# The instruction scheduler's timing model, in a float32 encoder on one core

## The chip, the cores and the metric

The kernel runs on one core of one Trainium2 chip. The metric is the device time of one execution in microseconds; smaller is better. The core has five instruction streams that run side by side and wait for one another through semaphores: PE (TensorE, matmuls; its weight loads are shown apart as PEld), DVE (VectorE), ACT (ScalarE), POOL (GpSimd) and SP (SyncE, which here issues most DMA transfers). Each stream is carried out strictly in the order in which the compiled program has it: an instruction that waits holds up all behind it on its engine.

## The reference

Two pre-norm residual layers over 512 tokens with 1024 features in float32, on a grid of 8 by 64 tokens. Layer 0 has grouped-query attention and latent attention side by side, layer 1 a neighbourhood attention with a window of 8 by 16 tokens. Each layer ends with an MLP of 4096 hidden features:

```python
for layer in range(DEPTH):                       # DEPTH = 2
    hn = rmsnorm(h, norm_mix[layer])
    if layer % 2 == 0:
        h = h + hybrid_attention(hn, ...)        # 8 + 8 heads, full softmax over 512 keys
    else:
        h = h + neighbourhood_attention(hn, ...) # 16 heads, gathered keys, learned bias
    u = jax.nn.relu(rmsnorm(h, norm_ffn[layer]) @ w_up)
    h = h + (u * u) @ w_down
return rmsnorm(h, final_norm)
```

## The kernel before

The residual stream is kept transposed on the chip as `hT` (features on the partitions, 8 blocks of 128 by 512 tokens). Every float32 operand of a matmul is split in two: a high part in the matmul's own format (`fp32r`), made by ACT, and the rest, made by DVE (or POOL) as a difference. A product of two such operands is three matmuls: high by high, high by rest, rest by high (`mm3` at lines 501 to 503). Weights come through `chunk` (line 183 on): SP loads a `raw` tile, ACT writes `whi` (line 212), DVE writes `wlo` (line 202). `weights` keeps up to five loads and two splits ahead of the matmul that asks for them.

The stages in the order of time are these:

- The projection of layer 0's inputs (`use_w`), with the norms, statistics and rotations that lead to the first heads (`ev_ka`, `ev_va`, `ev_q`, lines 593 to 710).
- `attend` for 16 heads in four blocks of 128 queries each: scores into a bank (line 997), a reduction on DVE (1001), an exponential on ACT (1003), a reciprocal on DVE (1004), a scaling on POOL (1005), transposes on PE (972), their split by ACT and DVE (974, 975), the product with the values (985). Between the steps `fill.run` writes pieces of other projections into the program, so many microseconds' worth a step.
- The output projection, then `mlp(0)`. A part of the MLP is done by products with seven multiplications in place of eight (class `Seven`): POOL forms sums of weight blocks (302 to 304), ACT and DVE split them (308, 309), PE multiplies (388 to 390), DVE combines the banks (397 to 400). The converse sums and splits of the activations (336 to 340, 362, 363) are written between the matmuls of the neighbouring products.
- `valuesC`, `projC` and `attend_C`, layer 1's attention, with the same kind of fillers.
- The output projection, `mlp(1)` with the last norm (`last_mlp`), and the stores.

The Python code writes one long list of instructions. As the `TileContext` closes, the framework turns it into the order of each engine. Its scheduler replays the list on a timing model: each time an engine comes free in the replay, it takes the earliest written instruction of that engine whose inputs, buffers and semaphores are ready in the replay at that moment. The order so found is the order that the chip executes. The semaphores are put in afterwards, so a wrong order costs waiting time, not correctness.

Three things limit the scheduler. The large slots (`a0` to `a29`) are taken and given back in Python, so which tile follows which in a slot is fixed as written. `tc.keep_in_program_order` (lines 630, 1184 and 1244) puts an instruction behind everything written before it on its engine: the conversions of activations in the MLPs are held so. And `attend_C` is written within

```python
return tc.manual_schedule(engines={mybir.EngineType.PE, mybir.EngineType.Activation, mybir.EngineType.DVE,
                                   mybir.EngineType.Pool})
```

which keeps the written order on four engines; SP's DMA issues are free there too. The pools with several buffers (`raw`, `whi`, `wlo`, `sc`, `p`, `ti`, and the eight PSUM banks under `mm`, `s`, `t`, `o`) are handed out as the replay reaches their users.

## Time and profile before

| | us |
|---|---|
| three runs | 1182.31, 1183.46, 1184.22 (median 1183.46) |
| profiled execution, first to last instruction | 1184.0 |
| PE idle in it, by stretches of the trace: 0 to 50 | 1.38 |
| 50 to 160 (end of the projection, start of the first attention) | 9.71 |
| 160 to 260 | 0.45 |
| 260 to 660 (first MLP, start of layer 1) | 0.23 |
| 660 to 820 (second attention) | 0.64 |
| 820 to 1080 (output projection, most of the second MLP) | 0.00 |
| 1080 to 1110 | 2.23 |
| 1110 to 1184 | 8.91 |

The profile's span runs from the first to the last instruction of one execution. A busy time is the union of an engine's instructions; matmuls overlap in the pipeline, so PE's busy time also holds slower stretches, which show in the distance between the starts of matmuls. In a row of the timeline stand the start, the time taken, the engine, the source line, the operation, the tile written and the tiles read with their shapes, the count, and in brackets how long the engine was idle before and what ended that.

### The profile page before, as it was taken

The page shows a single profiled execution, that of the slowest core. Times are in us where ns is not written, and L with a number is a line of the kernel's source. Part 1 is how long each engine was busy: PE and PEld are TensorE (multiplying, and loading weights), DVE is VectorE, ACT ScalarE, POOL GpSimd, SP SyncE. Part 2 cuts the span into 40 slices and gives each one's busy share as a digit, 9 for nine tenths or more (in the row PEclk, how much of TensorE's full clock was granted, in tenths as well). Part 3 has the DMA queues.
Part 4 walks back from the last instruction along what each step waited for, and adds up shares of the span by engine and source line. Part 5 has one row for each costly group of instructions (what it writes and reads, how often), then busy time and mean ns, then how long its engine had stood idle before and what let it go on. Part 6 is the DMA issues. An engine that isn't in the chain of part 4 may idle for free.

```text
span 1184.0 us, 19784 instructions
## 1 busy us (share of the span) xinstructions
PE 1160.5 (98%) x7128; PEld 1021.2 (86%) x7128; DVE 883.2 (75%) x1514; ACT 640.3 (54%) x1081; POOL 526.1 (44%) x662
## 2 busy tenths in 40 slices
PE   9989999999999999999999999999999999999997
PEld 8667778888899899988998998988889989998895
DVE  5788998878967368786884676667996736778975
ACT  4468676664546247562553565555554624666344
POOL 3267343224562377819602232231376625774710
PEclk9999999999999999999999999999999999999998
DMA  7223225212524723225226464433352341322412
GB/s 244 71 54 92 68 78 134 62 56 77 167 86 134 263 70 90 72 90 165 67 72 178 131 184 126 116 112 109 107 165 76 115 134 55 98 64 89 143 36 71
DMA packets 110145, 128.01 MB, mean 108 GB/s; under 512 B 9075, under 2 KB 86816, under 8 KB 110048
## 3 DMA queue, kind: packets, MB, share of 16 engines
q1 hardware_dynamic: 106992, 119.30, 33.5%
q0 software_dynamic: 2304, 6.31, 2.2%
q8 instruction: 56, 0.92, 0.3%
q10 hardware_dynamic: 752, 1.15, 0.3%
q14 instruction: 41, 0.34, 0.1%
HBM read 104.32 MB, written 6.29 MB: 93 GB/s over the span
## 4 chain that ended last, share of the span: by engine, by line
PE 81%; DVE 4%; ACT 1%; issue 1%; POOL 0%; DVEq 0%; ACTq 0%
PE mm L503 8%; PE mm L501 8%; PE mm L502 8%; PE mm L390 4%; PE mm L389 4%; PE mm L388 4%; PE t L388 3%; PE t L389 3%; PE t L390 3%; PE s L502 2%; PE s L503 2%; PE s L501 2%; PE s L390 2%; PE s L388 2%; PE s L389 2%; PE s L997 2%
## 5 line engine op out<-in xcount | busy, mean ns | idle before, releaser
L309 DVE TENSOR_TENSOR wlo<-a,whi 128x896 fp32r<-128x896 f32 x132 | 161.8, 1230 | 83.7 <-ACT whi L308 82.9
L308 ACT ACTIVATE whi<-a 128x896 fp32r<-128x896 f32 x132 | 125.0, 950 | 155.0 <-PE o L502 45.8
L501 PE MATMUL mm<-a,whi 128*128 128x512 f32 x485 | 195.9, 406 | 0.9 <-DVE a L915 0.7
L503 PE MATMUL mm<-a,wlo 128*128 128x512 f32 x485 | 192.1, 397 | 2.5 <-DVE wlo L202 2.5
L502 PE MATMUL mm<-a,whi 128*128 128x512 f32 x485 | 192.5, 397 | 0.1
L202 DVE TENSOR_TENSOR wlo<-raw,whi 128x1024 fp32r<-128x1024 f32 (+4 forms) x117 | 139.3, 1193 | 66.4 <-ACT whi L212 63.9
L212 ACT ACTIVATE whi<-raw 128x1024 fp32r<-128x1024 f32 (+3 forms) x120 | 116.4, 971 | 92.2 <-PE s L502 39.8
L302 POOL TENSOR_TENSOR a<-a 128x128 f32<-128x128 f32 x132 | 85.1, 645 | 173.3 <-DMA a<-in_ffn_w_up_dram 103.9
L303 POOL TENSOR_TENSOR a<-a 128x256 f32<-128x256 f32 x132 | 120.2, 910 | 10.3
L304 POOL TENSOR_TENSOR a<-a 128x128 f32<-128x128 f32 x132 | 115.1, 872 | 10.3
L503 PEld LDWEIGHTS mm<-a,wlo 128*128 128x128 f32 x485 | 91.7, 189 | 23.7 <-DVE wlo L202 3.4
L501 PEld LDWEIGHTS mm<-a,whi 128*128 128x128 f32 x485 | 91.8, 189 | 20.4 <-PE t L972 0.9
L502 PEld LDWEIGHTS mm<-a,whi 128*128 128x128 f32 x485 | 91.9, 190 | 17.4 <-DVE a L545 0.4
L388 PE MATMUL mm<-a,whi 128*128 128x256 f32 x370 | 103.9, 281 | 0.0
L389 PE MATMUL mm<-a,whi 128*128 128x256 f32 x370 | 103.9, 281 | 0.0
L390 PE MATMUL mm<-a,wlo 128*128 128x256 f32 x370 | 103.7, 280 | 0.0
L1005 POOL TENSOR_SCALAR p<-p,ti 128x512 f32<-128x512 f32 x64 | 46.2, 724 | 92.3 <-DVE ti L1004 81.1
L1430 POOL TENSOR_SCALAR p<-p,ti 128x256 f32<-128x256 f32 x64 | 35.6, 567 | 104.8 <-DVE ti L1429 91.8
L388 PE MATMUL t<-a,whi 128*128 128x256 f32 x264 | 74.2, 281 | 0.0
L389 PE MATMUL t<-a,whi 128*128 128x256 f32 x264 | 74.1, 281 | 0.0
L390 PE MATMUL t<-a,wlo 128*128 128x256 f32 x264 | 73.9, 280 | 0.0
L390 PEld LDWEIGHTS mm<-a,wlo 128*128 128x128 f32 x370 | 69.6, 188 | 0.2 <-DVE wlo L309 0.2
(338 smaller groups left out, 3210.8 us busy)
## 6 DMA issues: line engine op xcount, KB each, us to landing
a<-in_ffn_w_up_dram SPq DMA_DIRECT2D x104, 256.0 KB
raw<-in_ffn_w_down_dram SPq DMA_DIRECT2D x46, 512.0 KB
raw<-in_od_w_qkv_dram SPq DMA_DIRECT2D x64, 128.0 KB
a<-in_ffn_w_down_dram SPq DMA_DIRECT2D x28, 256.0 KB
raw<-in_ffn_w_up_dram SPq DMA_DIRECT2D x12, 512.0 KB
raw<-in_ev_w_in_dram SPq DMA_DIRECT2D x12, 384.0 KB
a<-a SPq DMA_DIRECT2D x18, 256.0 KB
bias<-bx SPq DMA_DIRECT2D x16, 256.0 KB
```

Source lines behind the costliest of these rows:

```text
L202: z = lambda: (eng or DVE).tensor_tensor(to, src, f32(high), op=ALU.subtract)
L212: ACT.activation(hi[:, 0:m], raw[:, 0:m], AF.Copy)
L303: POOL.tensor_tensor(r[:, 4:6], r[:, 2:3].to_broadcast([P, 2, P]), r[:, 0:7:6], op=ALU.add)
L304: POOL.tensor_tensor(r[:, 7], r[:, 3], r[:, 5], op=ALU.subtract)
L308: ACT.activation(hi[:, 0:896], raw[:, 128:1024], AF.Copy)
L309: DVE.tensor_tensor(lo[:, 0:896], raw[:, 128:1024], f32(hi[:, 0:896]), op=ALU.subtract)
L388: PE.matmul(o, wh, x[:, 0], start=kp == 0 and n in (0, 1, 3, 5), stop=False, skip_group_check=True)
L389: PE.matmul(o, wh, x[:, 1], start=False, stop=False, skip_group_check=True)
L390: PE.matmul(o, wl, x[:, 0], start=False, stop=kp == self.np - 1, skip_group_check=True)
L501: PE.matmul(o, wh, xh, start=first, stop=False)
L502: PE.matmul(o, wh, xl, start=False, stop=False)
L503: PE.matmul(o, wl, xh, start=False, stop=last)
```

## The change

One argument of the `TileContext` is set:

```diff
-    with tile.TileContext(nc) as tc:
+    with tile.TileContext(nc, schedule_with_timeline_sim=True) as tc:
         encoder_kernel(tc, aps, out)
```

Without it the scheduler replays the program on the framework's plain simulator of a core; with it, on the framework's timeline simulator, the more detailed of its two timing models. The written list, the pins, the hand-ordered stretch, the tiles and the instructions stay the same; the order of the instructions on each engine may differ wherever it is not pinned, and with it the order in which buffers of a pool are handed out.

## The prediction

> **What bounds the kernel now.** I read the page first, then the busy time by stretches, then what TensorE (PE) waited for, then the timelines around the longest of those waits.
>
> ```profile
> span 1184.0 us, 19784 instructions
> ...
> PE 1160.5 (98%) x7128; PEld 1021.2 (86%) x7128; DVE 883.2 (75%) x1514; ACT 640.3 (54%) x1081; POOL 526.1 (44%) x662
> ...
> PE 81%; DVE 4%; ACT 1%; issue 1%; POOL 0%; DVEq 0%; ACTq 0%
> ```
>
> PE works nearly all the time and carries most of the chain that ended last. No instruction is added or removed, so its work stays; only its 23.5 us of idle time (1184.0 - 1160.5) and what follows from idling can change. The next view says where that idle time lies: span of the stretch, then busy us and instructions of each engine, then the granted clock.
>
> ```profile
> 0.00:50.00 50.00, 48.62 (x235) 40.15 (x236) 29.28 (x60) 23.69 (x36) 14.19 (x21) 1.00 0.50 166
> 50.00:160.00 110.00, 100.29 (x548) 77.09 (x547) 95.76 (x236) 79.43 (x168) 57.06 (x59) 0.98 0.31 78
> 160.00:260.00 100.00, 99.55 (x572) 83.73 (x571) 83.11 (x180) 67.22 (x139) 30.28 (x39) 1.00 0.27 77
> 260.00:660.00 400.00, 399.77 (x2564) 361.64 (x2563) 293.94 (x399) 197.39 (x275) 199.77 (x252) 1.00 0.39 119
> 660.00:820.00 160.00, 159.36 (x982) 140.59 (x981) 108.29 (x290) 89.84 (x214) 44.27 (x79) 1.00 0.47 133
> 820.00:1080.00 260.00, 260.00 (x1665) 235.45 (x1664) 192.90 (x235) 138.56 (x184) 146.49 (x174) 1.00 0.33 102
> 1080.00:1110.00 30.00, 27.77 (x116) 22.25 (x115) 28.54 (x39) 10.97 (x16) 19.16 (x22) 0.94 0.32 97
> 1110.00:1184.00 74.00, 65.09 (x460) 60.28 (x459) 51.36 (x80) 33.21 (x55) 14.94 (x19) 0.96 0.23 71
> ```
>
> Of the idle time 9.71 us lie between 50 and 160 us (end of the first projection, start of the first attention), 2.23 between 1080 and 1110 (second MLP), 8.91 behind 1110 (nearly all the last output chain) and 1.38 ahead of 50 (first loads). The two long stretches from 260 to 660 and from 820 to 1080, the MLPs, idle 0.23 us together. The reader is to see that the MLPs can lose much and gain nothing, while the first attention can do either.
>
> **The change, part by part.** The scheduler replays the written program on a timing model. Whenever an engine comes free in that replay, it gets the earliest written instruction whose inputs and buffers are ready there. The change replaces the model, so what moves is which instruction counts as ready, on PE, ACT, DVE, POOL and on SP's DMA issues. Nothing else moves: the slots a0 to a29 are dealt out in the written order, the calls at lines 630, 1184 and 1244 pin some instructions behind the ones written before them, and the second attention (660 to 820) holds the order of its four engines by hand.
>
> *What can be gained.* PE's own waits:
>
> ```profile
> PE s L997 <- DVE ti L1001: 2.9, 2, 2.4
> PE mm L503 <- DVE wlo L202: 2.5, 2, 2.2
> PE t L597 <- POOL sc L595: 1.4, 3, 0.8
> PE s L997 <- DVE a L624: 1.4, 1, 1.4
> ```
>
> These are places where the present order puts an instruction ahead of its inputs. A model nearer to the chip would put other matmuls there. A wait also costs clock behind it; the two longest ones show that:
>
> ```profile
> 74.61 0.76 PE L997 MATMUL s<-a,a 128*128 128x512 f32 x2 [2.39 <-DVE ti L1001]
> ...
> 76.45 0.63 PE L503 MATMUL mm<-a,wlo 128*128 128x512 f32 x1
> 76.87 0.63 PE L501 MATMUL mm<-a,whi 128*128 128x512 f32 x1
> 77.30 0.63 PE L502 MATMUL mm<-a,whi 128*128 128x512 f32 x1
> ```
>
> ```profile
> 1099.72 0.39 PE L501 MATMUL mm<-a,whi 128*128 128x512 f32 x1
> 1099.95 0.40 PE L502 MATMUL mm<-a,whi 128*128 128x512 f32 x1
> 1102.58 0.79 PE L503 MATMUL mm<-a,wlo 128*128 128x512 f32 x1 [2.23 <-DVE wlo L202]
> 1103.17 0.63 PE L501 MATMUL mm<-a,whi 128*128 128x512 f32 x1
> ...
> 1105.73 0.52 PE L501 MATMUL mm<-a,whi 128*128 128x512 f32 x1
> ```
>
> Matmuls of 512 columns start 0.23 us apart before the wait and 0.43 after it. At 1102.58 the wait itself is 1102.58 - 1099.95 - 0.23 = 2.4 us; the seven steps to 1105.73 take 3.15 instead of 7 x 0.23 = 1.6, another 1.5. So a wait of this size is worth 2.4 + 1.5 = 3.9 us. The ceiling of the gain is then 9.71 + 0.02 x 110 = 11.9 us from 50 to 160 (idle time and the clock of 0.98) and 3.9 at 1102. I leave the ends alone: the first loads and the last chain of outputs have nothing beside them to put forward. Ceiling: about 16 us. What limits it is DVE, busy 95.76 of the 110 us: where PE no longer waits for one DVE result it soon waits for the next. From nothing to 11.9, I take a quarter for the first attention, 3 us.
>
> By a rule of the Trainium skill (TensorE: Matmul & The Clock Gate, section HAM oscillation) only PE gaps above about 3.4 us cost clock, so a new wait of 2.4 us would cost itself alone. The rows differ: 2.39 us of waiting were enough here. By the page three such waits would be 7.2 us instead of 11.7, and the sum below 1187.7.
>
> *What can be lost.* In the MLPs PE's next weights are split by ACT and DVE just ahead of use. The tight places are those where DVE also sums or converts:
>
> ```profile
> 469.63 1.82 DVE L830 TENSOR_TENSOR a<-a,a 128x512 fp32r<-128x512 f32 x2
> 471.37 1.62 DVE L309 TENSOR_TENSOR wlo<-a,whi 128x896 fp32r<-128x896 f32 x1
> ...
> 476.47 1.53 DVE L309 TENSOR_TENSOR wlo<-a,whi 128x896 fp32r<-128x896 f32 x1
> ```
>
> ```profile
> 473.05 0.39 PE L390 MATMUL s<-a,wlo 128*128 128x256 f32 x1
> ...
> 478.12 0.33 PE L390 MATMUL s<-a,wlo 128*128 128x256 f32 x1
> ```
>
> The first split ends at 472.99, and the matmul that reads it starts at 473.05; the second ends at 478.00, and its reader starts at 478.12. The cover is 0.06 to 0.12 us. If the new ranking puts one more evacuation or sum ahead of such a split, PE waits for the length of that instruction; if it puts a chain there, PE waits as at 1102.58:
>
> ```profile
> 1094.97 2.96 DVE L363 TENSOR_TENSOR a<-a,a 128x512 fp32r<-128x512 f32 x3
> ...
> 1101.05 1.47 DVE L202 TENSOR_TENSOR wlo<-raw,whi 128x1024 fp32r<-128x1024 f32 x1
> ```
>
> That split stood behind conversions (L363) and evacuations. Behind a late split stand the next evacuations and splits on DVE, and PE waits for them all; SP then issues the next load late:
>
> ```profile
> SPq L190 <- DVE wlo L202: 255.7, 66, 18.4
> SPq L300 <- DVE wlo L309: 162.9, 57, 12.0
> ```
>
> SP waits there for buffers to come free, and that is harmless now, as no load ends a wait of PE in the trace; were loads ranked late, POOL's sums would wait and then PE. The MLPs have five places of that kind: two where the first product ends in the sums (470 to 480, and the second layer's counterpart near 1030), two conversions of the up-product's raw results, and the norm near 830. A place costs between nothing and 3.9 us, and from below nothing is excluded as PE idles there 0.23 us in all. Seven such waits (27 us, the five and two at seams with the attention) are my far end. I take three, nearer to the row at 1102.58 than to the rows at 473: 3 x 3.9 = 11.7 us. The second attention I leave at zero, covered by its pinned order; only SP's issues move there.
>
> Sum against the profiled execution: 1184.0 - 3.0 + 11.7 = 1192.7 us; that execution lies 0.5 us above the median of 1183.46, so the forecast is **1192.2 us**, 0.7% slower.
>
> **The rivals.** *Faster.* The better replay sees that the scores at 74.61, the splits at 1102.58 and the statistics near 55 come late, and puts matmuls of the waiting projections there. For it: all three are misjudged ready times, and PE has independent matmuls beside them. Against it: DVE is busy 87% of that stretch. Half of the 16 us: 1175.5 us. It decides where more than half the ceiling comes back and at most one new wait of 3.9 us appears. Chance 0.32.
>
> *Nothing to be measured.* The order changes, but the MLPs stay in written order on PE and the splits stay paced by PE's buffers; or the flag changes next to nothing. About 1183.5 us, chance 0.16. Here, 0.2% (2.4 us) is about what a measurement can tell from no change.
>
> *Much slower, by DVE and POOL in each other's way.* Short DVE operations beside a POOL operation are long:
>
> ```profile
> 64.46 1.27 DVE L580 TENSOR_SCALAR rsQ<-rsQ 128x32 f32<-128x32 f32 x1
> ...
> 65.66 1.82 POOL L202 TENSOR_TENSOR wlo<-raw,whi 128x512 fp32r<-128x512 f32 x1
> ...
> 66.25 1.27 DVE L159 TENSOR_SCALAR ti<-rsQ 128x32 int32<-128x32 int32 x1
> ...
> 67.43 0.17 DVE L162 TENSOR_SCALAR ti<-rsQ 128x32 f32<-128x32 f32 x1
> ```
>
> The same small form takes 0.17 us alone and 1.27 beside POOL. A ranking that lines POOL's splits up with the statistics ahead of the attention, where every DVE step is waited for, pays 1.1 us a time; 18 times would be 20 us: 1203 us, chance 0.10. The Trainium skill (SBUF — State Buffer, section Who interferes with whom) says that DVE and GpSimd share one pair of ports under an exclusive lock, so that order decides who blocks. The trace agrees with 1.27 against 0.17 us.
>
> **How the numbers follow.** The forecast (three new waits, little gained) has 0.42, with 1186 to 1200 as its own range: 2.4 us above the median, and five waits (1183.5 - 3.0 + 19.5). Slower by over 0.2% is 0.42 + 0.10 = 0.52, within 0.2% is 0.16, faster is 0.32. The range runs from 1174, six tenths of the ceiling, to 1208, the far end of seven waits less the 3 us gained (1183.5 + 27.3 - 3.0).
>
> **What would show it.** Right: PE idle time from 260 to 660 and 820 to 1080 above 5 us, ended by wlo (L202, L309), with matmuls 0.43 us apart behind it; PE idle from 50 to 160 near 7 to 9 us. Wrong: those stretches still full and the first attention's idle time halved (faster), or both unchanged. Short DVE operations of over 1 us more often than now would speak for the port rival. A second attention that grows would mean that SP's order, which I left at zero, decides.

## The result, and the profile after

| | before | after |
|---|---|---|
| median, us | 1183.72 (1182.31 to 1184.22, 4 runs) | 1228.99 (1228.34 to 1229.38, 4 runs) |
| ratio, with its 95% interval | 1 | 1.0384 [1.0369, 1.0398] |
| profiled execution's span, us | 1184.0 | 1227.6 |

The kernel is 3.8% slower, by 45 us. The direction was the forecast's; the size was not, and the time lies outside the range.

The page of the kernel after, its busy times and the shares of the chain that ended last:

```profile
PE 1170.5 (95%) x7128; PEld 1027.9 (84%) x7128; DVE 873.1 (71%) x1514; ACT 639.1 (52%) x1081; POOL 524.5 (43%) x662
...
PE 84%; DVE 9%; issue 2%; POOL 2%; DMA 1%; ACT 1%; DVEq 0%; POOLq 0%; SPq 0%
```

The five engines' counts are those of before. PE's idle time went from 23.5 to 57.1 us (1227.6 - 1170.5), and its busy time rose by 10.0, as the matmuls behind the waits take longer (0.63 and 0.80 us in the rows below, otherwise 0.40). DVE's share of the chain grew from 4% to 9%. The busy time by stretches says where (span, then busy us and instructions of PE, PEld, DVE, ACT and POOL, the granted clock, the DMA share and GB/s):

```profile
50.00:160.00 110.00, 93.69 (x484) 69.78 (x485) 90.38 (x222) 71.82 (x150) 58.73 (x57) 0.98 0.26 68
...
310.00:335.00 25.00, 14.22 (x48) 10.30 (x47) 22.93 (x26) 16.91 (x31) 21.29 (x18) 0.73 0.20 64
335.00:660.00 325.00, 323.68 (x2189) 298.03 (x2188) 229.00 (x295) 154.20 (x199) 163.17 (x208) 1.00 0.37 113
...
890.00:918.00 28.00, 17.16 (x60) 12.60 (x59) 24.43 (x27) 17.91 (x32) 21.80 (x19) 0.76 0.17 57
918.00:1080.00 162.00, 162.00 (x1081) 148.64 (x1080) 104.39 (x124) 71.87 (x88) 90.34 (x116) 1.00 0.34 103
1080.00:1110.00 30.00, 30.00 (x256) 30.00 (x255) 23.16 (x27) 18.48 (x23) 23.28 (x29) 1.00 0.22 65
```

Two short stretches, 310 to 335 and 890 to 918, idle 10.8 us each, at clocks of 0.73 and 0.76. They are the same place in the two layers: the seam where the output projection hands over to the MLP's first product. The rest of both MLPs is as full as before (1.3 us idle from 335 to 660, none from 918 to 1080). The first attention idles 16.3 us where it idled 9.7. What PE waited for (total, times, longest):

```profile
PE mm L501 <- ACT a L833: 12.3, 2, 6.2
PE mm L501 <- DVE sc L1127: 9.2, 2, 4.6
PE t L530 <- DVE sc L661: 4.4, 1, 4.4
...
PE s L1426 <- DMA a<-a: 2.2, 1, 2.2
...
PE s L390 <- DVE wlo L309: 1.3, 2, 0.9
```

The weight splits, which the forecast had blamed ahead of time, end 1.3 us of waiting. The two longest groups, 21.5 us, are ended by the evacuation of the first product's banks (line 1127, and behind it the split at line 833 of the squared result).

**What happens at a seam.** The first product starts with plain products, which need no norm; their results stand in six PSUM banks until `rb`, the norm's factor, is known, because the evacuation at 1127 multiplies by it. The product behind them reads what these evacuations make. DVE's timeline there, kernel before (L931 adds a block of the output projection to the residual stream, L508 splits a block, L517 adds its square to the sums):

```profile
254.83 1.88 DVE L931 TENSOR_TENSOR hT<-hT,mm 128x512 f32<-128x512 f32 x3 [0.89 <-PE mm L503]
...
265.05 0.68 DVE L931 TENSOR_TENSOR hT<-hT,s 128x512 f32<-128x512 f32 x1
...
269.05 0.68 DVE L931 TENSOR_TENSOR hT<-hT,o 128x512 f32<-128x512 f32 x1
...
272.17 0.68 DVE L517 TENSOR_TENSOR acc<-acc,sc 128x512 f32<-128x512 f32 x1
...
279.58 0.16 DVE L169 SCALAR_TENSOR_TENSOR ti<-ti,ti 128x4 f32<-128x4 f32 x1
281.12 3.79 DVE L1142 SCALAR_TENSOR_TENSOR a<-hT,gT,rb 128x512 f32<-128x512 f32 x4 [1.37 <-ACT rb L1136]
```

The same, kernel after:

```profile
275.22 1.88 DVE L931 TENSOR_TENSOR hT<-hT,mm 128x512 f32<-128x512 f32 x3 [0.94 <-PE mm L503]
...
281.21 0.68 DVE L931 TENSOR_TENSOR hT<-hT,o 128x512 f32<-128x512 f32 x1
...
282.47 0.68 DVE L517 TENSOR_TENSOR acc<-acc,sc 128x512 f32<-128x512 f32 x1
283.07 1.41 DVE L508 SCALAR_TENSOR_TENSOR a<-hT,gT,a 128x512 fp32r<-128x512 f32 x2
284.40 1.22 DVE L202 TENSOR_TENSOR wlo<-raw,whi 128x1024 fp32r<-128x1024 f32 x1
...
292.33 2.14 DVE L517 TENSOR_TENSOR acc<-acc,sc 128x512 f32<-128x512 f32 x3
...
304.30 0.15 DVE L169 SCALAR_TENSOR_TENSOR ti<-ti,ti 128x4 f32<-128x4 f32 x1
...
310.30 3.78 DVE L1142 SCALAR_TENSOR_TENSOR a<-hT,gT,rb 128x512 f32<-128x512 f32 x4 [0.38 <-ACT rb L1136]
314.00 0.68 DVE L1127 SCALAR_TENSOR_TENSOR sc<-mm,rb 128x512 f32<-128x512 f32 x1
314.60 5.50 DVE L1142 SCALAR_TENSOR_TENSOR a<-hT,gT,rb 128x512 f32<-128x512 f32 x4
...
325.43 0.68 DVE L1127 SCALAR_TENSOR_TENSOR sc<-mm,rb 128x512 f32<-128x512 f32 x1
```

PE's timeline, kernel before (the two groups of matmuls that belong to the norm):

```profile
276.20 0.95 PE L522 MATMUL t<-ones,acc 128*128 128x1 f32 x8
...
279.80 0.65 PE L530 MATMUL t<-cst,ti 128*128 128x128 f32 x4 [0.22 <-DVE ti L169]
```

PE's timeline, kernel after:

```profile
299.58 0.95 PE L522 MATMUL t<-ones,acc 128*128 128x1 f32 x8
...
309.03 0.60 PE L530 MATMUL t<-cst,ti 128*128 128x128 f32 x4
...
313.41 0.39 PE L503 MATMUL o<-a,wlo 128*128 128x512 f32 x1
319.93 1.62 PE L501 MATMUL mm<-a,whi 128*128 128x512 f32 x2 [6.13 <-ACT a L833]
326.16 0.80 PE L501 MATMUL mm<-a,whi 128*128 128x512 f32 x1 [4.61 <-DVE sc L1127]
326.76 0.80 PE L502 MATMUL mm<-a,whi 128*128 128x512 f32 x1
...
329.49 1.32 PE L501 MATMUL mm<-a,whi 128*128 128x512 f32 x3
330.64 0.40 PE L501 MATMUL s<-a,whi 128*128 128x512 f32 x1
```

Read as a chain, from the end of the last addition to the residual stream to `rb`:

| step, us | before | after | longer by |
|---|---|---|---|
| last addition (L931) to the end of the sums of squares (L517) | 269.73 to 272.85: 3.1 | 281.89 to 294.47: 12.6 | 9.5 |
| to the column sums on PE (L522) | 276.20: 3.3 | 299.58: 5.1 | 1.8 |
| to the end of the root (L169) | 279.74: 3.5 | 304.45: 4.9 | 1.3 |
| to the broadcast on PE (L530) | 279.80: 0.1 | 309.03: 4.6 | 4.5 |
| to the first instruction that reads `rb` (L1142) | 281.12: 1.3 | 310.30: 1.3 | 0.0 |

The chain takes 28.4 us instead of 11.4, 17 more. Over half lies on DVE, which has all seven sums still to do behind the last addition, with splits (L202, L508) between them. In the kernel before four of the seven are done by then. There the eight additions come as the two halves of the output projection end on PE, four from 254.83 on and four from 265.05 on, with sums and splits between; after, the halves come out together, and the eight stand within 6.7 us (275.22 to 281.89). Most of the rest is PE, which does other matmuls first though the root is there (no wait stands in the L530 row). By then the plain products are soon done. The next matmul (319.93) reads an activation that ACT splits out of the first evacuated bank, and the one at 326.16 waits for a further bank, whose evacuation starts at 325.43, behind conversions on DVE. PE stops at 313.41 + 0.23 = 313.64, waits 6.3 us, does two matmuls in 1.6 us, waits 4.6, and then runs ten matmuls in 4.48 us (326.16 to 330.64) instead of 2.3. That is 6.3 + (1.6 - 0.5) + 4.6 + 2.2 = 14.2 us. Layer 1's seam does the same from 895 to 914, with waits of 6.2 and 4.6.

**A measure for what follows.** To line up kernels whose times differ, PE's lost time is taken per place: the distance from each matmul's start to the next, less the median distance of its shape in the kernel before, where that is positive; places are counted by the work that PE has done. Behind it stands the time from PE's last matmul to the end of the span.

| lost time of PE, us | before | after |
|---|---|---|
| first projection and first attention (up to 220 us of work) | 30.8 | 37.8 |
| end of that attention, output projection, first seam (to 280) | 1.0 | 16.8 |
| rest of the first MLP (to 560) | 2.5 | 4.3 |
| entry of the second attention (to 640) | 1.6 | 5.2 |
| second attention (to 760) | 4.2 | 4.2 |
| its end, output projection, second seam (to 840) | 2.0 | 17.2 |
| second MLP (to 1040) | 1.5 | 1.6 |
| the late split of before (1102.58), last products | 5.2 | 1.3 |
| behind the last matmul | 8.9 | 10.9 |

The differences add up to +41.6 of the span's 43.6 us; 31 of them are the two seams.

### The profile page after: what moved, and what is told of

The parts are those of the page before. It is cut to its first block, busy times and chain, and to the rows that moved or that the text cites. A ratio compares the mean times of both kernels' runs of the same rounds, so it can differ in the third digit from the quotient of the medians.

```text
span 1227.6 us, 19767 instructions
## 1 busy us (share of the span) xinstructions
PE 1170.5 (95%) x7128; PEld 1027.9 (84%) x7128; DVE 873.1 (71%) x1514; ACT 639.1 (52%) x1081; POOL 524.5 (43%) x662
## 4 chain that ended last, share of the span: by engine, by line
PE 84%; DVE 9%; issue 2%; POOL 2%; DMA 1%; ACT 1%; DVEq 0%; POOLq 0%; SPq 0%
PE mm L502 8%; PE mm L503 8%; PE mm L501 8%; PE mm L390 4%; PE mm L389 4%; PE mm L388 4%; PE s L501 3%; PE s L502 3%; PE s L503 3%; PE t L390 2%; PE t L388 2%; PE t L389 2%; PE s L390 2%; PE o L985 2%; PE s L388 2%; PE s L389 2%
## 5 line engine op out<-in xcount | busy, mean ns | idle before, releaser
L309 DVE TENSOR_TENSOR wlo<-a,whi 128x896 fp32r<-128x896 f32 x132 | 156.7, 1189 | 89.5 <-ACT whi L308 88.4
L501 PE MATMUL mm<-a,whi 128*128 128x512 f32 x485 | 190.1, 411 | 24.0 <-ACT a L833 12.3
L202 DVE TENSOR_TENSOR wlo<-raw,whi 128x1024 fp32r<-128x1024 f32 (+4 forms) x117 | 136.3, 1168 | 94.0 <-ACT whi L212 86.2
L302 POOL TENSOR_TENSOR a<-a 128x128 f32<-128x128 f32 x132 | 88.9, 673 | 251.9 <-DMA a<-in_ffn_w_up_dram 207.6
L502 PE MATMUL mm<-a,whi 128*128 128x512 f32 x485 | 194.0, 400 | 1.0 <-DVE a L508 1.0
L501 PEld LDWEIGHTS mm<-a,whi 128*128 128x128 f32 x485 | 93.0, 193 | 47.0 <-ACT a L833 13.2
L303 POOL TENSOR_TENSOR a<-a 128x256 f32<-128x256 f32 x132 | 124.1, 940 | 8.1
L304 POOL TENSOR_TENSOR a<-a 128x128 f32<-128x128 f32 x132 | 108.3, 820 | 8.1
L502 PEld LDWEIGHTS mm<-a,whi 128*128 128x128 f32 x485 | 92.7, 191 | 21.3 <-DVE a L508 1.8
L503 PEld LDWEIGHTS mm<-a,wlo 128*128 128x128 f32 x485 | 92.6, 191 | 20.7
L390 PE MATMUL mm<-a,wlo 128*128 128x256 f32 x370 | 99.8, 281 | 0.0
L1005 POOL TENSOR_SCALAR p<-p,ti 128x512 f32<-128x512 f32 x64 | 50.3, 790 | 99.4 <-DVE ti L1004 76.6
L389 PEld LDWEIGHTS mm<-a,whi 128*128 128x128 f32 x370 | 69.7, 188 | 0.2
```

Of the source, the lines that this page charges most:

```text
L202: z = lambda: (eng or DVE).tensor_tensor(to, src, f32(high), op=ALU.subtract)
L303: POOL.tensor_tensor(r[:, 4:6], r[:, 2:3].to_broadcast([P, 2, P]), r[:, 0:7:6], op=ALU.add)
L304: POOL.tensor_tensor(r[:, 7], r[:, 3], r[:, 5], op=ALU.subtract)
L309: DVE.tensor_tensor(lo[:, 0:896], raw[:, 128:1024], f32(hi[:, 0:896]), op=ALU.subtract)
L389: PE.matmul(o, wh, x[:, 1], start=False, stop=False, skip_group_check=True)
L390: PE.matmul(o, wl, x[:, 0], start=False, stop=kp == self.np - 1, skip_group_check=True)
```

## The experiments

The question was whose order carries the loss (PE's, that of DVE, ACT and POOL, or SP's), and where. All kernels but two set the flag of the change; all of these but one then give some engines, in some stretch of the program, the compiled order of the kernel before. The two without the flag get PE's order of the kernel after, and the one left over takes the written order. But for that one the edit is the same each time:

```diff
+def as_listed(tc, nc):
...
+    at = {i.name: i for i in nc.cur_bb.bb.instructions}
+    for part in zlib.decompress(base64.b85decode(_ORDER)).decode().split(";"):
+        names = [f"I-{n}" for n in part.split(",")]
+        for a, b in zip(names, names[1:]):
+            tc.add_manual_dep(at[b], a, mybir.DependencyInfo(mybir.DependencyClass.NoSync, mybir.DependencyReason.DATA),
+                              reason="as listed")
...
         encoder_kernel(tc, aps, out)
+        as_listed(tc, nc)
```

Each listed instruction is scheduled behind the one listed before it on its engine, without a semaphore. What differs is the list. It is written below as engines and stretches of the written program, in numbers of instructions (the code holds the packed numbers): up to 2876 goes the first attention, 2876 to 3378 the output projection and the plain products of layer 0 (the seam), 6646 to 7053 the entry of the second attention, 9120 to 9607 layer 1's seam, from 12680 the last outputs. Ratios are to runs of the kernel before on the same chip; what a run gives back is counted from the 1228.99 us above, across chips on which the medians of the kernel before lie within 0.5 us of each other.

**One engine's order for the whole program.**

```diff
+_ORDER: PE, whole program, as before
```

> The flag stays, but PE is held to the order that it has in the kernel before; the other engines are ranked by the new replay around it. Theory P (PE's order does it: the norm's matmuls L522 and L530 stand up to 90 places late and empty two seams of the MLPs): 1183 to 1195 us, and no PE wait above 3 us near 320 and 902. Rival V (the order on DVE, ACT and POOL does it: sums and splits ahead of the evacuations): above 1212 us, both waits still there. Rival S (SP's order of loads does it): above 1212 us too.

1206.16 us, ratio 1.0184 [1.016, 1.0207]. PE's order carries half of the loss, not all. The first seam loses nothing any more (1.1 us up to 280 instead of 16.8), although DVE is ranked by the new model; the second still loses some 3.5 us more than in the kernel before, about half of it in a wait of 1.7 us for the sums (L522). But the first attention loses 44.1 instead of 37.8: PE now waits where DVE and ACT follow the new order. SP is ranked by the new model here, so its order is not what empties the seams.

```diff
+_ORDER: DVE, ACT, POOL, whole program, as before
```

> The flag stays, but DVE, ACT and POOL are held to their order of before; PE and SP are ranked by the new replay. P: above 1205 us. V: below 1195 us. S: above 1212 us.

1229.54 us, 1.0384 [1.0354, 1.0414]: nothing gained in all, with other waits, as this row of PE's waits shows. The splits come in the old order, PE asks for them in the new. By place it is not the same kernel: the two seams lose some 14 and 7 us instead of 17 each, the first attention some 52 instead of 38.

```profile
PE mm L501 <- ACT whi L212: 8.3, 4, 3.1
```

```diff
+_ORDER: PE from 2876 on, as before
```

> The flag stays; PE is held to its order of before only from the first output projection on, and is free in the first projection and the first attention. P with the loss put where the trace of after shows it: the two seams and the entry of the second attention come back (some 33 us), the first attention keeps its 9: 1192 to 1200 us. If the first attention's order carries more than its own waits: above 1203 us.

1209.54 us, 1.0216 [1.0188, 1.0243], above what was expected. The second seam's stretch loses 5.5 us instead of 17.2 and the first's 7.6 instead of 16.8; most of that 7.6 lies at the border of the list, which is looked at further down. Behind the border PE idles 0.2 us from 270 to 340 of that run, where the rest of the first seam lies, with DVE free.

```diff
-    with tile.TileContext(nc, schedule_with_timeline_sim=True) as tc:
+    with tile.TileContext(nc) as tc:
+_ORDER: PE, whole program, as after
```

> The converse: the old timing model, with PE held to the order that it has in the changed kernel. P: 1215 to 1230 us, with both seam waits. V and S: 1184 to 1195 us.

1241.36 us, 1.0482 [1.0462, 1.0503]: PE's new order among the other engines' old order is worse than the change itself, with 19.8 and 18.1 us lost around the seams and 47.8 in the first attention. PE's order by itself brings the losses along.

**The seams by themselves.** The next two move only the 304 matmuls of the two layers' plain products, in both directions.

```diff
+_ORDER: PE, 3089 to 3378 and 9318 to 9607, as before
```

> The flag stays; PE is held to its order of before in the two products of 512 and 256 columns of each layer's MLP alone (304 of its 7096 instructions), which puts the norm's matmuls back by 53 and 80 places in the first layer and 47 and 75 in the second. Theory P, place: the two waits near 320 and 902 (14.4 and 15.2 us of lost PE time) go, 1196 to 1205 us. Rival V2 (the sums reach PE late because DVE makes them late; then PE only waits at L522 instead): above 1212 us.

1218.69 us, 1.0297 [1.0282, 1.0313]. It gives back 10.3 us (1228.99 - 1218.69), and a new wait takes the place of the old: the output projection ahead has the new order still, and the sums come late. PE's timeline:

```profile
295.27 1.87 PE L522 MATMUL t<-ones,acc 128*128 128x1 f32 x8 [5.24 <-DVE acc L517]
```

```diff
-    with tile.TileContext(nc, schedule_with_timeline_sim=True) as tc:
+    with tile.TileContext(nc) as tc:
+_ORDER: PE, 3089 to 3378 and 9318 to 9607, as after
```

> The converse: the old timing model, with PE held in those 304 instructions to the order of the changed kernel. P, place: 1209 to 1217 us, the two waits alone. V2: below 1195 us, since the sums are early here.

1200.16 us, 1.0145 [1.013, 1.016]: these 304 matmuls in the new order cost 16.5 us in a kernel that is otherwise the kernel before (8.0 and 8.6 us lost more at the two seams). PE's timeline shows the wait behind the plain products, now 5.12 us.

```profile
305.08 1.22 PE L501 MATMUL mm<-a,whi 128*128 128x512 f32 x2 [5.12 <-ACT a L833]
```

Both halves of the chain are thereby seen by themselves, as lost time above that of before: the late norm on PE costs 8.0 and 8.6 us a seam with DVE's sums on time; the late sums on DVE cost 10.2 and 9.4 (11.2 and 11.4 lost in the run ahead of this one) with PE's plain products on time. Together they cost 15.8 and 15.2, less than their sum, as one delay hides part of the other.

That the sums are late on DVE doesn't make it DVE's order that is wrong. In the runs with PE in its old order from 2876 on, and for the whole program, DVE is ranked by the new model, and the last sum ends 4.3 us behind the last addition in layer 0, where it was 12.6 (7.5 in layer 1, where it was 12.6). What is put back there, and not in the run with the plain products alone, is PE's order in the output projection.

**Written order instead of the old one.** The first listed order was one that the scheduler had found. Here PE keeps the order of the Python code, in the output projections of both layers and in the plain products.

```diff
-    for c in range(2):
-        out_proj(w_out, 4, ok, [4 * c + j for j in range(4)], None)
+    with tc.manual_schedule(engines={mybir.EngineType.PE}):
+        for c in range(2):
+            out_proj(w_out, 4, ok, [4 * c + j for j in range(4)], None)
...
-                plain()
+                with tc.manual_schedule(engines={mybir.EngineType.PE}):
+                    plain()
```

> The flag stays; PE alone keeps the written order within the last output projection of each attention and the two plain products behind it. Theory A (the late sums come from PE finishing the two halves of the output projection together, the rest from the place of the norm's matmuls): both seam waits go, 1197 to 1204 us. Theory B (DVE's own order makes the sums late): PE waits for them at L522 instead, as in e5, 1209 to 1219 us.

1218.05 us, 1.0288 [1.0272, 1.0303], a time of theory B, but with the waits of theory A. PE doesn't wait at L522: the last sum ends 4.3 us behind the last addition in layer 0, and the waits of 6.2 and 4.6 us are gone from both seams. The written order has costs of its own. The broadcast (L530) stands directly behind the column sums (L522), and PE waits there for the root, in both layers (2.7 and 2.8 us); and the start of the two output projections loses some 7 and 4 us more than in the kernel before. PE's waits show the first:

```profile
PE t L530 <- DVE ti L169: 5.5, 2, 2.8
```

```diff
+_ORDER: DVE, ACT, POOL, 2876 to 3378 and 9120 to 9607, as before
```

> The flag stays; DVE, ACT and POOL are held to their order of before from the last output projection to the end of the two plain products of each layer; PE is ranked by the new replay (the norm's matmuls then stand 20 and 52 places late in the first layer, 0 and 31 in the second). A: 1212 to 1224 us, the sums stay late. B: 1199 to 1208 us, the sums are early and the rest of the seam shrinks.

1216.07 us, 1.0265 [1.0247, 1.0284]: the other side alone gives back 12.9 us, a time of theory A. Yet the sums are early, as theory B had it (3.1 us behind the last addition in layer 0); PE waits for weights instead, 3.1 us between the two halves of each layer's additions, and in layer 0 once more for 3.3. The first in its timeline:

```profile
282.26 0.50 PE L501 MATMUL mm<-a,whi 128*128 128x512 f32 x1 [3.14 <-ACT whi L212]
```

**Both sides together.**

```diff
+_ORDER: PE, DVE, ACT, POOL, SP, 2876 to 3378 and 9120 to 9607, as before
```

> The changed kernel with all five engines in the old order in the two stretches from the last output projection of a layer to the end of its plain products, the rest free. Theory A (the loss at the seams is the order of several engines together, made for one another): the seam losses of 14 to 15 us each go whole and nothing takes their place, 1229 - 29 = 1200 us, 1195 to 1204. Rival B (what is late at the seams was already made late by the order of the attention in front of them): 1210 to 1222, with a wait left ahead of the plain products.

1204.85 us, 1.0184 [1.0166, 1.0203]: 24.1 us back, just above the range of theory A. The first stretch still loses 7.6 us instead of 1.0 (the border, below), the second 2.7 instead of 2.0.

```diff
+_ORDER: PE, DVE, 2876 to 3378 and 9120 to 9607, as before
```

> The two seams with only TensorE and VectorE in the old order, ScalarE, GpSimd and SyncE free. If the late norm matmuls on TensorE and the late sums of squares on VectorE are both halves of the loss (A): as with all five engines, 1196 to 1206. If ScalarE's splits or SyncE's loads carry a part (B): 1208 to 1218, with a wait of TensorE for a weight split.

1205.98 us, 1.019 [1.0175, 1.0206], within 1.1 us of the run with five engines. So ACT, POOL and SP need not be held. DVE's order adds little to PE's. By the lost time from 244 to 285 us of work, behind the border, the first seam loses 0.7 us here, 0.9 with PE alone (the run with PE from 2876 on) and 15.3 in the kernel after; from 795 to 845 the second loses 0.7 here, 3.9 with PE alone and 16.5 in the kernel after. So the seams are PE's order, output projection included; DVE's adds some 3 us in layer 1.

**The first attention and the entry of the second.**

```diff
+_ORDER: PE, DVE, ACT, POOL, SP, up to 2876, as before
```

> The flag stays; all five engines are held to their order of before in everything up to the first output projection, and ranked by the new replay behind it. If what is lost in the first attention stays there (about 9 us): 1216 to 1222 us. If its order also brings about the two seam waits: below 1205 us.

1214.88 us, 1.0264 [1.0249, 1.028]: the first attention is worth 14.1 us, of which the measure of lost time shows 11.1, 8.7 of them (37.8 - 29.1) in that place. Both seams lose what they lost (16.2 and 16.1).

```diff
+_ORDER: PE up to 900, as before
```

> The flag stays; PE is held to its order of before in the first projection and its statistics alone (335 instructions). If the first attention's loss of 14 us (e7) starts with the wait of 4.4 us for the key's norm at L530: 1213 to 1218 us. If that wait is one of many: 1221 to 1225 us. If PE waits for the same results elsewhere: no change from 1229.

1227.81 us, 1.0367 [1.0349, 1.0384], 1.2 us back. Putting PE alone back around the 4.4 us wait at L530 moved the wait and took little away.

```diff
+_ORDER: PE, DVE, ACT, POOL, SP, up to 2876; PE, 2876 to 3378, 6646 to 7053, 9120 to 9607, as before
```

> The flag stays; held to the order of before are all five engines up to the first output projection, and PE alone in both output projections with the plain products and at the entry of the second attention. If these places hold the whole loss: 1178 to 1184 us, with the gain near 1102 kept. If something else is lost: above 1187 us.

1198.26 us, 1.0119 [1.0103, 1.0135]. With only PE put back at the second attention's entry, no wait of PE for the transfer `a<-a` is left, so it was PE's order that made it late. The place gains nothing by it, though: just ahead of it PE in its old order now waits for activations that ACT and DVE split in the new one (1.1 us at L1386, 0.8 at L1388), and loses some 7 us where the kernel after lost 5. Of the seams, the first has its loss at the border again (PE idles 3.7 us from 240 to 262). Behind it PE is full, though DVE has all eight products with `rb` (L1142) ahead of two weight splits, where the kernel before has four, a split, four, a split: PE waits for neither split. The second has a wait for the sums left. The busy time by stretches, and a row of PE's waits:

```profile
285.00:300.00 15.00, 15.00 (x66) 12.03 (x66) 14.83 (x13) 6.50 (x13) 14.19 (x11) 1.00 0.18 56
...
PE t L522 <- DVE acc L517: 1.7, 1, 1.7
```

**Is that all of it?**

```diff
+_ORDER: PE, DVE, ACT, POOL, SP, up to 2876, 2876 to 3378, 6646 to 7053, 9120 to 9607, as before
```

> As before, and also all five engines in the old order up to the first output projection and where the second attention begins; free are the rest of both MLPs, the second attention and the last outputs. Theory A (three places carry the loss, each as an order of all engines): 1229 - 29 - 14 - 4 = 1182 us, 1178 to 1188. Rival B (the free order of the MLPs itself costs some waits more, as in the runs where one engine alone was put back): 1192 to 1200.

1189.76 us, 1.005 [1.0033, 1.0066], between the two theories. The lost time shows one place left, 7.2 us ahead of the first seam. PE's timeline there has the attention's last products (L985) with nothing between them, and then a wait at the first matmuls of the output projection:

```profile
256.19 1.22 PE L501 MATMUL mm<-a,whi 128*128 128x512 f32 x2 [2.06 <-ACT a L833]
```

In the kernel before, output projection matmuls stand between these steps. They belong to the next list, and the two lists were not tied to each other, so the new model placed them apart.

```diff
-_ORDER: ... up to 2876, 2876 to 3378, ...
+_ORDER: ... up to 3378, ...
```

> As the kernel with all three places in the old order, but the first layer up to the end of its plain products is one list instead of two, so that matmuls of the output projection may stand among the attention's last steps again. Theory A (the 6 us lost there, around 250 to 262 us of that run, are matmuls that could not cross the border between the two lists): 1189.8 - 6.3 = 1183.5 us, 1180 to 1186; TensorE's wait of 2.1 us for a converted h at L833 is gone. Rival B (they come from the free MLP behind it): 1188 to 1191, the wait stays.

1184.38 us, 1.0003 [0.9994, 1.0012]: the border was it, the wait is gone, and the kernel is level with the kernel before. With the flag set and the MLPs free, the three places are the whole net loss; the 2 us that the last quarter still gains (below) may hide as much lost elsewhere.

```diff
-_ORDER: ... 6646 to 7053, 9120 to 9607, ...
+_ORDER: ... 6646 to 9607, ...
```

> As that one, and the second attention with the seam behind it is one list too, so that the new order is free in the two MLPs and the last outputs alone. If the second attention's free order costs nothing (A): the same as the kernel with one list in the first layer, within 2 us, 1180 to 1185. If its border costs as the first layer's did, though less (B): 1 to 3 us faster than that kernel, 1178 to 1182, and ahead of the kernel before by 0.1 to 0.4%.

1182.65 us, 0.9993 [0.9985, 1.0002]: not told apart from the kernel before, and 1.7 us from the run ahead of it, as theory A had it.

**Where the gain at 1102 went.**

```diff
+_ORDER: PE, DVE, ACT, POOL, SP, up to 9607, as before
```

> The flag stays; all five engines are held to their order of before up to the second layer's norm and its two plain products, and ranked by the new replay in the rest of the last MLP (the last quarter). There the trace of after lacks the wait at 1102.58 of before (4.1 us of lost PE time): 1178 to 1182 us, faster than before. If the gain there hangs on what comes ahead of it: 1183 to 1187 us.

1182.28 us, 0.999 [0.998, 0.9999], just above the first range. The late split is gone (1.4 us lost in the last products instead of 5.2), and yet only 1.4 us came of it. The end of the span tells why. In the kernel after, the timeline of the last products (PE, DVE, and ACT's issues of the last stores) reads:

```profile
1215.16 0.40 PE L1635 MATMUL mm<-whi,a 128*128 128x512 f32 x1
1215.40 0.40 PE L1634 MATMUL s<-wlo,a 128*128 128x512 f32 x1
...
1216.32 0.39 PE L1635 MATMUL s<-whi,a 128*128 128x512 f32 x1
1216.34 0.68 DVE L1587 TENSOR_TENSOR a<-a,mm 128x512 f32<-128x512 f32 x1
...
1221.80 0.55 ACTq L1610 DMA_DIRECT2D out_dram<-a  x1
```

Seven of the last bank's twelve matmuls were put ahead of the end of the third bank, so only five (1215.40 to 1216.32) stand behind it. Both banks end within 1.2 us (1215.16 and 1216.32), their last chains run side by side on DVE and ACT, and the last store is issued 5.5 us behind the last matmul's start. The last run puts that part back too, and leaves the second MLP alone to the new model.

```diff
+_ORDER: PE, DVE, ACT, POOL, SP, up to 9607, from 12680 on, as before
```

> The kernel that leaves only the last quarter free, with the last chains of outputs in the old order too, so that free is the second MLP alone. In the new order TensorE takes seven matmuls of the last bank ahead of the end of the third, the last two outputs are finished side by side, and the span ends 10.9 us behind the last matmul instead of 8.9. Theory A (4.0 us are gained at the late split and 2.0 given back at the last outputs): 1182.3 - 2.0 = 1180.3 us, 1179 to 1181.5, 0.2 to 0.4% ahead of the kernel before, and 8.8 to 9.0 us behind the last matmul. Rival B (the end of the span is set by the stores, whatever the chains do): 1182 to 1183.5 us.

1179.79 us, 0.9973 [0.9963, 0.9983]: faster than both kernels. Its timeline at the same place:

```profile
1170.55 0.39 PE L1635 MATMUL s<-whi,a 128*128 128x512 f32 x1
...
1174.89 0.55 ACTq L1610 DMA_DIRECT2D out_dram<-a  x1
```

Only the fourth bank is left to finish. The last store is issued 4.3 us behind the last matmul's start, and the span ends 8.9 us behind its end, as in the kernel before (10.9 in the kernel after). The new model's order is worth 4 us at the late split and cost 2 us in the last outputs.

## Why the prediction was right in direction and wrong in size

**What bounds the kernel: right.** The MLP stretches could lose and not gain. They lost, but nearly all of it in two places of some 17 us that the view of the stretches, cut at 260 and 820, did not single out.

**The gain of 3 us in the first attention: wrong sign.** Its idle time was to fall to 7 to 9 us between 50 and 160; it rose from 9.7 to 16.3, and putting that place back is worth 14.1 us. The wait at 74.61 went, but one of 4.4 us came in the statistics (L530 behind L661).

**The gain of 3.9 us at 1102: right, and not booked.** The lost time there fell by 3.9 us, the ceiling's number. The sum left it out, and it left "the ends alone", where 2.0 us were given back.

**The loss of 11.7 us: this is the step that failed.** It looked for the loss at the weight splits, and took three of five places at 3.9 us each. PE idles in 260 to 660 and 820 to 1080 as the sign asked (10.8 + 1.3 us from 310 to 660 alone), but not ended by `wlo`: those waits come to 1.3 us. Of the five places only "the norm near 830" was one that matters; its twin in layer 0 near 280 was not on the list, and each cost 14 to 15 us where a place was to cost 3.9 at most. The price came from one late split, behind which PE is served at once. Behind the norm's factor stand six PSUM banks and the whole next product, and the chain of 11 us that leads to it was late on two engines in turn: 9.5 us on DVE and 6.3 on PE (1.8 + 4.5), by PE's order in the main. With 2 x 15 us there, and 7 + 2 for the first attention and the entry of the second, the sum would have been some 39 us and the time 1222. That the kernel came out slower, as forecast, is luck as far as the weight splits go; only the premise that a full stretch can lose and not gain held.

**The second attention at zero: nearly right.** Inside, it loses 4.2 us as before. At its entry PE waits 2.2 us for SP's `a<-a`. That was not SP's order, as the prediction would have read it, but PE's: with PE put back the wait is gone, though others take its place.

**The rivals.** *Faster* asked that more than half of the ceiling come back; only the 3.9 us at 1102 did. *Nothing* fell. *DVE and POOL in each other's way* fell too: of the 392 DVE operations on at most 64 columns, 4 took over 1 us before and 3 after, and their times add up to 58.8 us before and 57.3 after. Nor is a short DVE operation beside POOL long as a rule: before, 61 of them began well inside a POOL operation, and 57 of these took under 0.3 us.

**The step from the span to the time** was off by about 2 us as well. It set the span of 1184.0 against the median of the times. In the runs here the time lies 1.7 to 2.1 us above the span (1229.38 against 1227.6), so that execution of before was some 2.5 us above its median rather than 0.5.

**Why the new model orders so** is only inferred. On POOL, the sums of lines 302, 303 and 304 belong together, and the second and third read what the one ahead wrote. In the trace of before all 140 such triples run on POOL without another instruction between; after, 100 of 140 do. The timeline of POOL after shows one that doesn't:

```profile
316.98 0.90 POOL L302 TENSOR_TENSOR a<-a 128x128 f32<-128x128 f32 x1
317.84 1.72 POOL L336 TENSOR_TENSOR a<-a 128x512 f32<-128x512 f32 x1
319.51 1.19 POOL L338 TENSOR_TENSOR a<-a,a 128x256 f32<-128x256 f32 x1
320.66 1.76 POOL L303 TENSOR_TENSOR a<-a 128x256 f32<-128x256 f32 x1
...
326.06 0.97 POOL L304 TENSOR_TENSOR a<-a 128x128 f32<-128x128 f32 x1
```

The mean from the start of a first sum to the end of its third rose from 2.6 to 3.2 us, the longest from 3.9 to 10.0. It looks as though the detailed model holds a result back from its own engine for a while, so that the next written step of another chain counts as ready first; the same might put PE's two halves of the output projection side by side, and other matmuls ahead of the norm's. No run here shows the replay's own times, so this stays open.

## What to carry to other kernels

The orders of the engines are made for one another: putting back one engine's for the whole program returned half at best and made new waits, while PE and DVE together at two places returned 23 of the 45 us, and a stretch must be tied to the one ahead of it or the border costs 5 us (1189.76 against 1184.38). The engine on which a chain is late need not be the one whose order is wrong: the sums were late on DVE, and PE's order of the output projection brought them back. When a scheduler's ranking changes, look first at short chains across several engines on whose one result a whole row of buffers waits (here the norm, with six banks behind it); price such a place by how much later the whole chain can end (here 17 us, for 14 to 15 us of PE's time), not by one instruction. A scheduler's model can be used where it helps alone: the detailed one in the second MLP, the old order elsewhere, is 0.27% faster than the kernel before.

## What was not expected of the hardware

A step on DVE that reads the sum just written by DVE costs little extra: three dependent additions of 128x512 took 2.14 us (the row at 292.33), where three of the same size into different blocks, out of PSUM banks, took 1.88 (the row at 275.22). That is 0.13 us a step (2.14 - 1.88, over two steps), which is about all that an order could win here by putting other work between such steps.

After a wait of 4.6 us the first two matmuls start 0.6 us apart (326.16, 326.76, 327.35) and the next five 0.43, before they are 0.23 apart again from 330.64 on. The price of that wait is the wait and 2.2 us. In layer 1, behind a wait of the same 4.6 us, the spacing of 0.43 lasts until 914.09 instead, and it is the wait and 2.9 us.
